# A decoder trunk in fp32 pieces: when the attention stage reads back its softmax weights, its biases and its turned heads

## The chip, the cores and the metric

One core of one Trainium2 chip runs the whole program. The metric is the device time of one launch, in microseconds (us); of several runs the median counts. Beside it stands one profiled execution, from which every busy time and every wait below comes.

## What is computed

The reference is a decoder trunk over 256 tokens of 2048 channels: a gated linear attention layer, a gated feed-forward layer with a short causal convolution, a softmax attention layer that reads shared keys and values, and a second feed-forward layer. The change lies in the third part, which with 256 tokens is plain causal attention over one block (16 heads of 128 channels):

```python
kv = rms_norm(x, norm_w) @ w_kv
k, v = jnp.split(kv, 2, axis=-1)
k = rms_norm(k.reshape(B, S, H, Dh), k_norm_w)
...
q = (rms_norm(x, norm_w) @ w_q).reshape(B, S, H, Dh)
q = (rms_norm(q, q_norm_w) * (Dh ** -0.5)).transpose(0, 2, 1, 3)
...
s_own = jnp.einsum('bhqd,bhkd->bhqk', q_c, k_own).astype(jnp.float32)
s_own = s_own + bias_table[:, rel_bucket(dist_own)][None]
s_own = jnp.where(dist_own >= 0, s_own, -jnp.inf)
p = jax.nn.softmax(scores, axis=-1)
o = einsum(p, v)                  # then  o @ w_out  and the residual
```

## The kernel before

**Weights in two parts, one step at a time.** All products are fp32 and are made from pieces: every weight tile `w` is split into `whi` (ScalarE, L140) and `wlo = w - whi` (VectorE, L141). `WeightStream` holds the list of all weight tiles in the order of use. `step()` hands out the next 128x1024 tile; a counter `cur` counts these steps, and it is the clock of the whole program. In the attention stage a step is 12 matmuls of 512 columns: 8 with `whi` (L290) and 4 with `wlo` (L293). `whi` and `wlo` have three buffers each, so the splits run at most a few steps ahead of TensorE.

**Side work is hung on the step counter.** `after(n, job)` puts a job into a list that `step()` empties when `cur` has come `n` steps further. Jobs that are due at the same step run in the order in which they were entered. `ws.behind()` places what a job issues on ScalarE and VectorE behind the newest weight split in that engine's queue. What the text of the program leaves open is decided when it is compiled: each engine gets one fixed queue of instructions, and an instruction that writes a new tile has its place in the queue only where a buffer for it is there.

**Slots.** One pool, `big`, has 35 buffers ("slots") of 4 KB per partition. Nearly all that lives longer than a moment is in it: the operands `xkv` (8), the four `bias` tiles, the turned heads `q0`, `q1`, `k0`, `k1`, the evacuated products `hsq`, `q`, `k`, `vm0`, `vm1`, the tiles `z` and `turned` of the transposition, the softmax weights `p0`, `p1`, the outputs `ox`.

**The attention stage** has 96 steps of products, counted here from its start:

- steps 0 to 31, query heads, four groups of eight steps (four heads each); steps 32 to 63, key heads, four groups; steps 64 to 95, values, four groups. Each group sums in one of three PSUM tiles `acc`. After it comes the product with the output weights, `mo`.
- A query or key group is evacuated by `head_norm` (L876 to L884: two squares and two scaled copies on ScalarE, a reduction on VectorE, a power on GpSimd, a product), transposed in 32x32 blocks (L384), stored to DRAM (`store`, L387, on GpSimd's DMA queue) and read back turned (`load`, L393, four DMAs). This is `turned(...)`, and `through(g, z, jobs)` times it: the store 1 step after the group, the load 2 steps after, and the reading job 8 steps after. That job is `features` (L892, L896, L303, L304): it makes the operands `q0`, `q1` or `k0`, `k1`.
- `softmax(hd)` for the heads of key group g is due 10 + i steps after the group: scores on TensorE (L908, L910), bias, maximum, exponential, sum, scaling, and block transposition. Two heads make a pair, and a pair goes through DRAM as well: store, load 2 steps after, and `spread_weights` 8 and 9 steps after, which makes `p0` and `p1` (L303, L304, L938).
- `v_out` evacuates a value group (L360, L361, L367), `values(v, p)` (L371 to L374) multiplies the weights of pair p with the values, 3 and 4 steps after the group, and splits the result into `ox` (L303, L304). For pairs 1 and 3, which the output product takes in a form with seven products in place of eight, it also copies the result (`ow`, L956) and makes four sums of its parts (`combine`, L603 to L606, and a split).
- The biases come from a small product (`bias_inputs`, `bias_rows`) that is written to DRAM, and four loads of 512 KB (`bias_load`, L866), at steps 6, 13, and 20, 24, 28, 32. Loads of `hf` (L970) and the operands `xkv` are due at steps 18 to 21 and 26 to 33.

GpSimd's DMA queue carries all of these stores and loads, and GpSimd computes the powers between them; a DMA that has to wait holds up what is behind it. The weights come by SyncE's queue.

Of the kernel before, what the change touches and what calls it, by code (L numbers as in the profile page):

```python
# [8 lines left out]
F32 = mybir.dt.float32  # L9
# [9 lines left out]
S = 256  # L19
# [138 lines left out]
def trunk(ctx: ExitStack, tc: tile.TileContext, xT, x_tok, cst, msk, w1p, w2a, w_k, w_qa, w_v2, w_v, w_g, w_go,  # L158
# [14 lines left out]
    def slot(shape, dt, name):  # L173
        return big.tile(shape, dt, name=name, tag="slot")

    def temp(name, shape=(128, 2, S), dt=F32):
        return tmp.tile(list(shape), dt, name=name, tag="temp")
# [8 lines left out]
    ws = WeightStream(tc, raw, parts)  # L186
# [18 lines left out]
    kqw = keep.tile([128, 1], F32, name="kqw")  # L205
# [60 lines left out]
    cur = [0]  # L266
    later = []

    def after(steps, job):
        later.append((cur[0] + steps, job))  # L270
# [84 lines left out]
    xs = rows(nrm.xs)  # L355
# [7 lines left out]
    def v_out(v, ps, n):  # L363

        r0, r1 = (n.col[:, t:t + 1] for t in range(2))
        split_rows(v[0], ps[:, 0, :], r0)
        A.activation(v[1], ps[:, 1, :], AF.Copy, scale=r1)  # L367
# [8 lines left out]
    def turned(name, groups, a=4, t=2):  # L376

        scratch_ = dram.tile([groups, 4, 32, 4, a * t * 32], F32, name=name)

        def fresh():  # L380
            return slot([128, 4, a, t, 32], F32, "z")

        def square(z, src, t):
            V.transpose(z[:, :, :, t].rearrange("p q a c -> p a q c"), src.rearrange("p (a q c) -> p a q c", q=4, c=32))  # L384

        def store(g, z):
            nc.gpsimd.dma_start(scratch_[g].rearrange("i r q x -> (i r) (q x)"),  # L387
                                z.rearrange("p q a t c -> p (q a t c)"))

        def load(g):  # L390
            f = slot([128, 4, a * t * 32], F32, "turned")
            for q in range(4):
                nc.gpsimd.dma_start(f[32 * q:32 * q + 32], scratch_[g][:, :, q].rearrange("i r x -> r i x"))  # L393
            return f.rearrange("p i (a t c) -> p a t i c", a=a, t=t)

        def through(g, z, jobs):
            got = {}
            after(1, lambda: store(g, z))
            after(2, lambda: got.update(f=load(g)))

            def run(job):
                with ws.behind():
                    job(got["f"])

            for lag, job in jobs:
                after(lag, lambda job=job: run(job))

        return fresh, square, through
# [66 lines left out]
    for hd in (2, 3):  # L475
        ps = gemm_tok(xs)
# [66 lines left out]
    fresh, square, through = turned("keys", 2)  # L543
    for g in range(2):
        z = gemm_tok(xs, 1, lambda ps: evacuated(ps, nrm.col))
# [42 lines left out]
    fresh, square, through = turned("queries", 2)  # L588
    for g in range(2):
        z = gemm_tok(xs, 1, lambda ps: evacuated(ps, col16))  # L590
        jobs = []
# [7 lines left out]
    def combine(k, halves_, into):  # L599

        (a0, a1), (b0, b1) = halves_
        t = temp("comb", (128, 4, 128))
        V.tensor_add(t[:, 0], a1, b1)  # L603
        V.tensor_sub(t[:, 1], t[:, 0], a0)
        V.tensor_sub(t[:, 2], a0, a1)
        V.tensor_sub(t[:, 3], b0, t[:, 1])  # L606
        c = slot([128, 4, 2, 128], F32R, "comb")
        split(c[:, :, 0], c[:, :, 1], t)
        into[k] = c
# [253 lines left out]
    def bias_load(g):  # L863
        t = slot([128, 4, S], F32, "bias")
        s = bscr[:]
        nc.gpsimd.dma_start(t, bass.AP(tensor=s.tensor, offset=s.offset + 4 * g * 384,  # L866
                                       ap=[[1, 128], [384, 4], [1, S]]))
        bias.append(t)
# [21 lines left out]
    def features(x, f, scale, t0):  # L890

        A.activation(f[0].rearrange("p a (i c) -> p a i c", i=4), x[:, :, 0], AF.Copy, scale=scale)  # L892
        for c in range(2):
            w = temp("feat", (128, 2, S - 128 * t0))
            for i in range(2):
                A.activation(w[:, i].rearrange("p (t i c) -> p t i c", i=4, c=32), x[:, 2 * c + i, t0:], AF.Copy,  # L896
                             scale=scale)
            split(f[1][c][:, :, 0, :], f[1][c][:, :, 1, :], w)
# [5 lines left out]
    def softmax(hd):  # L904
        (q0, q1), (k0, k1) = qf[hd // 4], kf[hd // 4]
        q1, k1 = q1[hd // 2 % 2][:, hd % 2], k1[hd // 2 % 2][:, hd % 2]
        sp = bank("s", (128, 384))
        T.matmul(sp[:, 0:128], q0[:, hd % 4, :], k0[:, hd % 4, :], start=True, stop=True)  # L908
        for i, (a, b) in enumerate(((0, 0), (0, 1), (1, 0))):
            T.matmul(sp[:, 128:384], q1[:, a, :], k1[:, b, :], start=i == 0, stop=i == 2)  # L910
        s = temp("s", (128, 384))
        st = small.tile([128, 4], F32, name="st")
        bt = bias[hd // 4][:, hd % 4, :]
        for t, (c0, c1) in enumerate(((0, 128), (128, 384))):
            n = c1 - c0
            rev = bass.AP(tensor=bt.tensor, offset=bt.offset + n - 1, ap=[bt.ap[0], [-1, n]])
            V.tensor_tensor_reduce(s[:, c0:c1], sp[:, c0:c1], rev, -1.0, 3.0e38, OP.add, OP.min,
                                   st[:, t:t + 1])
            A.activation(s[:, c0:c1], s[:, c0:c1], AF.Exp, bias=st[:, t:t + 1], scale=-1.0,
                         accum_out=st[:, 2 + t:3 + t])  # L920
        V.reciprocal(st[:, 2:4], st[:, 2:4])
        for t, (c0, c1) in enumerate(((0, 128), (128, 384))):
            V.tensor_scalar(s[:, c0:c1], s[:, c0:c1], st[:, 2 + t:3 + t], None, op0=OP.mult)
        if hd % 2 == 0:
            pts.append(prob_z())
        prob_square(pts[-1], s, hd % 2)
        if hd % 2:
            prob_through(hd // 2, pts[-1], [(8 + i, lambda f, i=i: spread_weights(hd - 1 + i, f[:, :, i]))
                                            for i in range(2)])

    def spread_weights(hd, f):
        if hd % 8 == 0:
            p1s.append(slot([128, 8, 128], F32, "p1"))
        if hd % 2 == 0:
            p0s.append(slot([128, 2, 2, S], F32R, "p0"))
        hi, lo = (p0s[-1][:, hd % 2, i].rearrange("p (a i c) -> p a i c", a=2, i=4) for i in range(2))
        split(hi, lo, f[:, :2])
        A.copy(p1s[-1][:, hd % 8].rearrange("p (i c) -> p i c", i=4), f[:, 2])  # L938
# [3 lines left out]
    def values(v, p):  # L942
        if p < 6:
            op = bank("o", (128, 2, S))
        else:
            lent[:] = lent or acc_pair()
            op = lent.pop(0)
        for i in range(2):
            hd = 2 * p + i
            p0 = p0s[p][:, i]  # L950
            mix(op[:, i, :], v, (hd % 4) * 128, p0[:, 0], p0[:, 1], p1s[hd // 8][:, hd % 8])
        o = slot([128, 2, 2 * S], F32R, "ox")
        split(o[:, :, :S], o[:, :, S:], op)
        if p in sevens("mo"):
            w = temp("ow")
            A.copy(w, op)  # L956
            combine(p, [(w[:, i, :128], w[:, i, 128:]) for i in range(2)], ox_sums)
        ox.append(o)

    xkv = []  # L960
    after(6, bias_inputs)
    after(13, bias_rows)
    for g in range(4):
        after(20 + 4 * g, lambda g=g: bias_load(g))
    hf = []

    def fetch(m):
# [9 lines left out]
    for g in range(4):  # L977
        z = gemm_tok(xs, 1, lambda ps: head_norm(ps, "q"))
        if g % 2 == 0:
            q8 = slot([128, 8, 128], F32, "q0")  # L980
        q1 = slot([128, 4, 2, 128], F32R, "q1")
        f = (q8[:, g % 2 * 4:g % 2 * 4 + 4], (q1[:, 0:2], q1[:, 2:4]))
        qf.append(f)
        head_through(g, z, [(8, lambda x, f=f: features(x, f, 1.0, 1))])
    xs = rows(xkv)
    for g in range(4):
        z = gemm_tok(xs, 1, lambda ps: head_norm(ps, "k"))
        if g % 2 == 0:
            k8 = slot([128, 8, 128], F32, "k0")
        f = (k8[:, g % 2 * 4:g % 2 * 4 + 4], [slot([128, 2, 2, S], F32R, f"k1{c}") for c in range(2)])  # L990
        kf.append(f)
        head_through(4 + g, z, [(8, lambda x, f=f: features(x, f, kqw, 0))])
        for i in range(4):
            after(10 + i, lambda i=i, g=g: softmax(4 * g + i))
    for g in range(4):
        ps = gemm_tok(xs)
        if g % 2 == 0:
            vm1 = slot([128, 2, 512], F32, "vm1")
        v = (slot([128, 2, 512], F32R, "vm0"), vm1[:, g % 2, :])
        v_out(v, ps, n_q)  # L1000
        for c in range(2):
            after(3 + c, lambda v=v, p=2 * g + c: values(v, p))

# [108 lines left out]
```

## Time and profile before

| | us |
|---|---|
| median of 3 runs | 2206.23 |
| the three runs | 2205.48, 2206.23, 2217.24 |
| the profiled execution, its own time | 2213.89 |
| its span, first to last instruction | 2212.1 |
| TensorE busy in the span | 2180.5 |
| VectorE, ScalarE, GpSimd busy | 1596.1, 1283.9, 300.0 |

The profiled execution has 1.8 us outside its span, and it took 7.66 us more than the median of the three runs. In a timeline, a row gives the start, the length, the engine, the line, the operation with `out<-in`, how many instructions are merged in the row, and in brackets how long the engine had been idle and what ended that. "PE" is TensorE's matmuls, "ACT" ScalarE, "DVE" VectorE, "POOL" GpSimd. The attention stage's first query matmul starts at 1098.34 us, the first key matmul at 1195.36, the first value matmul at 1292.56, and the last one ends at 1388.82.

### The profile page before, as it was taken

The numbers are of one execution on the slowest core, as the hardware profiler recorded it, in microseconds if no ns is written. First come the engines' busy times: TensorE is split into PE (matmuls) and PEld (weight loads), VectorE is DVE, ScalarE is ACT, GpSimd is POOL, SyncE is SP. The second block draws the span as 40 slices with busy tenths as digits, with TensorE's granted clock in tenths as the row PEclk, the third lists the DMA queues.
The fourth block names the chain that finished last, engine by engine and source line by source line (L and its number), as shares of the span: only waits on it lengthen the run. The fifth ranks groups of instructions, "written<-read, shape, count | busy, mean of one in ns | idle before, by whom it ended". The sixth has DMA issues, their size and how long they took to land. (4 is left out here: it accounts for less than half of the span.)

```text
span 2212.1 us, 26963 instructions
## 1 busy us (share of the span) xinstructions
PE 2180.5 (99%) x9693; PEld 1798.9 (81%) x9693; DVE 1596.1 (72%) x2190; ACT 1283.9 (58%) x1856; POOL 300.0 (14%) x448
## 2 busy tenths in 40 slices
PE   9999999999999999999999999899999999999999
PEld 7888887888888888788887788788888888887787
DVE  6655677677777677978767677776777776779886
ACT  6555665555556565555466566555565565655554
POOL 1011111111111111010023231011111111110000
PEclk9999999999999999999999999999999999999999
DMA  8466577677787878576668677486777777775655
GB/s 314 175 228 209 192 243 244 212 233 250 230 254 237 246 238 244 183 245 222 225 229 305 214 253 235 167 259 203 239 244 235 250 242 241 237 246 190 229 209 171
DMA packets 92105, 510.11 MB, mean 231 GB/s; under 512 B 13714, under 2 KB 14754, under 8 KB 41923
## 3 DMA queue, kind: packets, MB, share of 16 engines
q1 hardware_dynamic: 60578, 417.53, 54.8%
q0 software_dynamic: 30816, 90.28, 15.3%
q8 instruction: 76, 1.25, 0.2%
q10 hardware_dynamic: 576, 0.58, 0.1%
q14 instruction: 59, 0.48, 0.1%
HBM read 463.22 MB, written 45.11 MB: 230 GB/s over the span
## 5 line engine op out<-in xcount | busy, mean ns | idle before, releaser
L141 DVE TENSOR_TENSOR wlo<-wraw,whi 128x1024 fp32r<-128x1024 f32 (+1 forms) x786 | 929.6, 1191 | 450.7 <-ACT whi L140 425.2
L140 ACT CAST whi<-wraw 128x1024 fp32r<-128x1024 f32 (+1 forms) x786 | 798.7, 1026 | 668.4 <-PE acc L290 425.0
L290 PE MATMUL acc<-whi,xw 128*128 128x512 f32 x3840 | 954.6, 390 | 3.6 <-ACT whi L140 3.1
L290 PEld LDWEIGHTS acc<-whi,xw 128*128 128x128 f32 x3840 | 721.7, 188 | 155.3 <-ACT whi L140 4.6
L293 PE MATMUL acc<-wlo,xw 128*128 128x512 f32 x1920 | 515.7, 390 | 0.0
L293 PEld LDWEIGHTS acc<-wlo,xw 128*128 128x128 f32 x1920 | 361.1, 188 | 75.1
L728 PE MATMUL acc<-whi,hid 128*128 128x512 f32 x572 | 182.5, 391 | 2.8 <-DVE c L769 2.0
L728 PE MATMUL p<-whi,hid 128*128 128x512 f32 x506 | 166.3, 390 | 0.0
L290 PE MATMUL acc<-whi,xkv 128*128 128x512 f32 x512 | 130.6, 394 | 5.1 <-ACT whi L140 5.1
L667 POOL DMA_DIRECT2D upT<-turned x176 | 114.3, 656 | 145.5 <-DMA turned<-z 56.7
L140 ACT CAST whi<-t 128x1024 fp32r<-128x1024 f32 x82 | 85.6, 1051 | 74.4 <-PE p L728 40.1
L728 PEld LDWEIGHTS acc<-whi,hid 128*128 128x128 f32 x572 | 106.8, 188 | 26.8 <-DVE c L769 2.9
L661 POOL DMA_DIRECT2D turned<-z x44 | 34.2, 776 | 679.4 <-DVE z L657 632.5
L290 PEld LDWEIGHTS acc<-whi,xkv 128*128 128x128 f32 x512 | 96.2, 190 | 25.4 <-ACT whi L140 6.0
L728 PE MATMUL acc<-whi,comb 128*128 128x512 f32 x328 | 108.0, 394 | 5.0 <-ACT whi L140 5.0
L676 ACT ACTIVATE au<-upT,cs 128x256 f32<-128x256 f32 x176 | 96.0, 595 | 27.1 <-DMA upT<-turned 26.9
L728 PEld LDWEIGHTS p<-whi,hid 128*128 128x128 f32 x506 | 94.9, 188 | 19.7
L141 DVE TENSOR_TENSOR wlo<-t,whi 128x1024 fp32r<-128x1024 f32 x82 | 99.0, 1218 | 5.8 <-ACT whi L140 4.4
L728 PE MATMUL acc<-wlo,hid 128*128 128x512 f32 x286 | 94.9, 391 | 2.0 <-DVE wlo L141 2.0
L680 DVE SCALAR_TENSOR_TENSOR au<-upT,cs,au 128x255 f32<-128x255 f32 x176 | 77.2, 472 | 16.3 <-ACT au L676 16.1
L728 PE MATMUL p<-wlo,hid 128*128 128x512 f32 x253 | 83.6, 389 | 0.0
L760 POOL DMA_DIRECT2D c<-rows x24 | 21.2, 1053 | 450.7 <-DVE c L755 438.5
(251 smaller groups left out, 1952.8 us busy)
## 6 DMA issues: line engine op xcount, KB each, us to landing
wraw<-w_up SPq DMA_DIRECT2D x176, 1024.0 KB, 5.3
wraw<-w_dn SPq DMA_DIRECT2D x88, 1024.0 KB, 5.0
turned<-z POOLq DMA_DIRECT2D x44, 512.0 KB, 3.5
upT<-turned POOLq DMA_DIRECT2D x176, 128.0 KB, 5.1
wraw<-w_g SPq DMA_DIRECT2D x16, 1024.0 KB, 5.3
wraw<-w_go SPq DMA_DIRECT2D x16, 1024.0 KB, 6.5
wraw<-w_mq SPq DMA_DIRECT2D x16, 1024.0 KB, 5.8
wraw<-w_kk SPq DMA_DIRECT2D x16, 1024.0 KB, 6.6
```

What stands on the lines that cost most here:

```text
L140: one = nc.scalar.copy(hi[:, a:b], src[:, a:b])
L141: two = nc.vector.tensor_sub(lo[:, a:b], src[:, a:b], hi[:, a:b].bitcast(F32))
L290: T.matmul(ps[:, t, :], xs(kt)[:, x0 + 128 * t:x0 + 128 * t + 128], hi[:, c:c + 512], start=kt == 0 and x0 == 0, stop=False)
L293: T.matmul(ps[:, t, :], xs(kt)[:, 128 * t:128 * t + 128], lo[:, c:c + 512], start=False, stop=kt == KT - 1)
L661: nc.gpsimd.dma_start(turned[J].rearrange("(a i) r q c -> (i r) a (q c)", a=4), z.rearrange("p (a q) t c -> p a (q t c)", a=4))
L667: nc.gpsimd.dma_start(f[32 * q:32 * q + 32].rearrange("p a (i c) -> p (a i) c", i=4), turned[J][:, :, q, :].rearrange("a r c -> r a c"))
L676: A.activation(au[:, i, :], t[:, i, :], AF.Identity, bias=col(cb + n), scale=col(cw + 2 * 2 * FT + n))
L680: V.scalar_tensor_tensor(au[:, i, 1:], t[:, i, :S - 1], col(cw + 2 * FT + n), au[:, i, 1:], op0=OP.mult, op1=OP.add)
L728: T.matmul(p[n], x[xi], w[wi][:, 512 * f:512 * f + 512], start=n not in begun, stop=left[n] == 0)
L760: nc.gpsimd.dma_start(r[n], res(n // 2, 2 * b + n % 2), accum_op=OP.add)
```

## The change

Every operation stays; what changes is when some of them are due, and the pool of one tile.

1. `through` takes the step of the load as an argument. Softmax pairs are now loaded 10 steps before the step at which `values` needs them and spread 4 and 3 steps before it (`use`). With the softmax two steps later (below), pair p of key group g is due to be stored at step 54 + 8g or 56 + 8g, loaded at 65 + 8g or 66 + 8g, spread from 71 + 8g or 72 + 8g, and used at 75 + 8g or 76 + 8g.
2. The biases: inputs at step 18 in place of 6, the product at 25 in place of 13, the four loads at 42, 50, 58, 66 in place of 20, 24, 28, 32.
3. Turned query heads are read 11 steps after their group in place of 8, turned key heads 10 steps after in place of 8, and the softmax starts 12 steps after the key group in place of 10.
4. A value group is evacuated inside `gemm_tok`, ahead of the next weight splits, in place of behind them. The tiles `vm0` and `vm1` are named before the product.
5. The copy `ow` takes a slot in place of one of the six `temp` buffers, and the four sums of pairs 1 and 3 come two steps later, behind the newest weight split.

```diff
-        def through(g, z, jobs):
+        def through(g, z, jobs, fetch=2):
             got = {}
             after(1, lambda: store(g, z))
-            after(2, lambda: got.update(f=load(g)))
+            after(fetch, lambda: got.update(f=load(g)))
...
         if hd % 2:
-            prob_through(hd // 2, pts[-1], [(8 + i, lambda f, i=i: spread_weights(hd - 1 + i, f[:, :, i]))
-                                            for i in range(2)])
+            use = values_at[0] + 8 * (hd // 4) + hd // 2 % 2 - cur[0]
+            prob_through(hd // 2, pts[-1], [(use - 4 + i, lambda f, i=i: spread_weights(hd - 1 + i, f[:, :, i]))
+                                            for i in range(2)], use - 10)
...
         if p in sevens("mo"):
-            w = temp("ow")
+            w = slot([128, 2, S], F32, "ow")
             A.copy(w, op)
-            combine(p, [(w[:, i, :128], w[:, i, 128:]) for i in range(2)], ox_sums)
+
+            def sums():
+                with ws.behind():
+                    combine(p, [(w[:, i, :128], w[:, i, 128:]) for i in range(2)], ox_sums)
+
+            after(2, sums)
         ox.append(o)

     xkv = []
-    after(6, bias_inputs)
-    after(13, bias_rows)
+    values_at = [cur[0] + 64 + 8 + 3]
+    after(18, bias_inputs)
+    after(25, bias_rows)
     for g in range(4):
-        after(20 + 4 * g, lambda g=g: bias_load(g))
+        after(42 + 8 * g, lambda g=g: bias_load(g))
...
-        head_through(g, z, [(8, lambda x, f=f: features(x, f, 1.0, 1))])
+        head_through(g, z, [(11, lambda x, f=f: features(x, f, 1.0, 1))])
...
-        head_through(4 + g, z, [(8, lambda x, f=f: features(x, f, kqw, 0))])
+        head_through(4 + g, z, [(10, lambda x, f=f: features(x, f, kqw, 0))])
         for i in range(4):
-            after(10 + i, lambda i=i, g=g: softmax(4 * g + i))
+            after(12 + i, lambda i=i, g=g: softmax(4 * g + i))
     for g in range(4):
-        ps = gemm_tok(xs)
         if g % 2 == 0:
             vm1 = slot([128, 2, 512], F32, "vm1")
         v = (slot([128, 2, 512], F32R, "vm0"), vm1[:, g % 2, :])
-        v_out(v, ps, n_q)
+        gemm_tok(xs, 1, lambda ps: v_out(v, ps, n_q))
         for c in range(2):
             after(3 + c, lambda v=v, p=2 * g + c: values(v, p))
```

## The prediction

> **What bounds the kernel now.** The page's busy times come first.
>
> ```profile
> span 2212.1 us, 26963 instructions
> PE 2180.5 (99%) x9693; PEld 1798.9 (81%) x9693; DVE 1596.1 (72%) x2190; ACT 1283.9 (58%) x1856; POOL 300.0 (14%) x448
> ```
>
> TensorE is busy for all but 31.6 us of the span, and no matmul is added or taken out. So the change can give back only time in which TensorE stood still or ran slowly, and only in the attention stage, which it touches. The second view is the list of TensorE's waits, cut to the value and output part of that stage (total, number, longest):
>
> ```profile
> PE o L371 <- ACT vm L360: 3.9, 2, 3.5
> PE p L728 <- DVE ox L304: 0.6, 1, 0.6
> PE p L728 <- DVE wlo L141: 0.5, 1, 0.5
> PE o L373 <- DVE vm L361: 0.4, 1, 0.4
> PE acc L374 <- ACT vm L367: 0.3, 1, 0.3
> PE o L374 <- ACT vm L367: 0.2, 1, 0.2
> ```
>
> These are 5.9 us, nearly all of it for values that came late out of PSUM. The third view is TensorE's timeline over the query and key groups, and beside it one key group of eight steps without a stop, as the windows show it:
>
> ```profile
> 1195.36:1217.12 21.76, 21.76 (x98) 18.02 (x96) 18.25 (x27) 16.07 (x29) 5.44 (x6) 1.00 0.78 271
> ```
> ```profile
> 1179.98 2.73 PE L290 MATMUL acc<-whi,xw 128*128 128x512 f32 x8 [2.38 <-ACT whi L140]
> 1184.22 2.22 PE L290 MATMUL acc<-whi,xw 128*128 128x512 f32 x8
> 1187.20 1.98 PE L290 MATMUL acc<-whi,xw 128*128 128x512 f32 x8
> ...
> 1228.60 2.12 PE L290 MATMUL acc<-whi,xkv 128*128 128x512 f32 x8 [0.45 <-ACT whi L140]
> 1231.46 1.98 PE L290 MATMUL acc<-whi,xkv 128*128 128x512 f32 x8
> ...
> 1252.63 3.55 PE L290 MATMUL acc<-whi,xkv 128*128 128x512 f32 x8 [4.69 <-ACT whi L140]
> 1257.08 1.98 PE L290 MATMUL acc<-whi,xkv 128*128 128x512 f32 x8
> ```
>
> A clean step takes 21.76 / 8 = 2.72 us. Three times TensorE waits for a weight split: 2.38, 0.45 and 4.69 us, together 7.52. After a stop it is also slow: the steps from 1179.98, 1184.22, 1228.60 and 1252.63 take 4.24, 2.98, 2.86 and 4.45 us, which is 1.52 + 0.26 + 0.14 + 1.73 = 3.65 us over a clean pace. The two together are 11.2 us. The fourth view, ScalarE's timeline, says why the split was late:
>
> ```profile
> 1177.57 0.63 ACT L892 ACTIVATE q<-turned 128x512 f32<-128x512 f32 x1 [5.62 <-DMA turned<-heads]
> ...
> 1226.19 0.63 ACT L892 ACTIVATE q<-turned 128x512 f32<-128x512 f32 x1 [5.05 <-DMA turned<-heads]
> ...
> 1247.64 1.70 ACT L896 ACTIVATE feat<-turned,kqw 128x256 f32<-128x256 f32 x4 [7.16 <-DMA turned<-heads]
> ```
>
> Each stop of TensorE follows a read of turned heads for which ScalarE stood still, with the next weight splits queued behind it. Three buffers of weights hide the first 3 us or so of such a wait, the rest reaches TensorE.
>
> The last view is when products leave PSUM. TensorE starts the group behind the last key group at 1292.56, and the one behind the first value group at 1316.26:
>
> ```profile
> 1292.56 1.98 PE L290 MATMUL acc<-whi,xkv 128*128 128x512 f32 x8
> ```
> ```profile
> 1316.26 1.98 PE L290 MATMUL acc<-whi,xkv 128*128 128x512 f32 x8
> ```
> ```profile
> 1317.62 0.68 ACT L876 ACTIVATE hsq<-acc,col_n 128x512 f32<-128x512 f32 x1
> ```
> ```profile
> 1351.99 0.68 ACT L360 ACTIVATE vm<-acc,col_n 128x512 fp32r<-128x512 f32 x1
> ```
> ```profile
> 1319.38 2.19 POOL L393 DMA_DIRECT2D turned<-probs  x4 [6.28 <-issue]
> ...
> 1330.59 2.20 POOL L393 DMA_DIRECT2D turned<-heads  x4 [3.33 <-ACT whi L140]
> ...
> 1354.91 2.29 POOL L393 DMA_DIRECT2D turned<-probs  x4 [6.60 <-DMA probs<-z]
> ```
>
> The evacuations begin 25.1 and 35.7 us after their products were complete, 9 and 13 steps late, and not because ScalarE waited in front of them (their rows have no bracket). Each stands within 3 us of the load of a softmax pair, 1319.38 and 1354.91, and that load is the last slot user before it in the program (due at steps 63 and 71, the evacuations at 64 and 72). I read this as follows: slots are given out in program order, so a load that must wait for its store to land also pushes back every later instruction that takes a slot. The lateness grows from group to group until values are multiplied in the middle of the output product.
>
> **The change part by part.** *Turned heads.* The reads of query heads move 3 steps (3 x 2.72 = 8.16 us) later, those of key heads 2 steps (5.44 us). The query waits of 5.62 and 5.05 us are under 8.16 and go. For the key read, 7.16 us is over 5.44, but its chain also starts sooner:
>
> ```profile
> 1228.58 1.23 DVE L141 TENSOR_TENSOR wlo<-wraw,whi 128x1024 fp32r<-128x1024 f32 x1 [3.41 <-ACT whi L140]
> 1229.73 1.30 DVE L384 STREAM_TRANSPOSE z<-k 128x512 f32<-128x512 f32 x2
> ```
>
> The transposition of this group stood behind a VectorE wait of 3.41 us that came from ScalarE's wait of 5.05. With that gone, the margin is 5.44 + 3.41 - 7.16 = 1.7 us. Against it goes the bias: its load is now due at the same step as the load of the key group (42 + 8g) and stands ahead of it in the queue. Its price lies between nothing, when the queue is waiting for the store anyway, and its whole landing time:
>
> ```profile
> bias<-bscr POOLq DMA_DIRECT2D x4, 512.0 KB, 6.5
> ```
>
> Nearest is the first end, since the key load has to wait for its own store several us after that step. I take 2 us; what remains of the wait is then about 0.3 us, and the buffers hide it. At the other end 4.8 us of wait would remain, up to 2 us of it on TensorE. In the query part the bias loads and the bias product leave the crowded stretch, which can only help the loads of `hf` there; I count nothing. Gain: 11.2 us.
>
> *Pairs kept in DRAM, softmax later.* The pair loads are now due 9 to 12 steps after their store is due, so none waits for its store, and the evacuation behind it keeps its place. What stands ahead of an evacuation now is the load of the key group, due 2 steps after that group. In the rows above it is issued 1330.59 - 1317.62 = 13 us, not quite 5 steps, after its group's evacuation, ahead of the next one at 8 steps. The softmax pairs between them are held to that point, one to three steps late, and they have 19 steps to their use. No operation is added, and GpSimd's queue carries the same stores and loads in another order.
>
> *Values, operand sums.* Evacuated in time, the first six pairs are multiplied inside the value groups (steps 75 to 92), and only the last two fall into the output product, as the program has it. This takes away the waits for `vm`, and the work around them at the low clock:
>
> ```profile
> 1366.54 0.28 PE L371 MATMUL o<-p,vm 128*128 128x256 f32 x1
> ...
> 1367.70 0.39 PE L908 MATMUL s<-k,q 128*128 128x128 f32 x2
> ```
> ```profile
> 1397.83 0.58 PE L371 MATMUL o<-p,vm 128*128 128x256 f32 x1 [3.52 <-ACT vm L360]
> ...
> 1402.69 0.92 PE L728 MATMUL p<-whi,ox 128*128 128x512 f32 x2
> ```
>
> One pair takes 1367.70 - 1366.54 = 1.16 us at the full clock; the two pairs from 1397.83 took 4.86, so 2.5 us were lost. Gain: 5.9 + 2.5 = 8.4 us. Evacuating ahead of the splits puts two ScalarE copies of 0.68 us and one VectorE operation in front of the next split; the buffers of weights hide 1.4 us, and without them it would cost four times that, 5.4 us. The sums two steps later go behind the splits and are due well before the steps of those pairs in the output product; `ow` only changes its pool. Nothing for these.
>
> *The sum.* 11.2 + 8.4 = 19.6 us against the profiled 2213.89, which leaves 2194.3. That execution was 7.66 us over the median of 2206.23. If this excess lies in the very stalls that go, the new median is also about 2194; if it lies elsewhere, 2206.2 - 19.6 = 2186.6. Nothing shown decides it; I take the middle, 2190.4, and add 1.6 us for waits that come up in a stage with other orders in all its queues: 2192.
>
> The clock term can be weighed against the Trainium skill, "TensorE: Matmul & The Clock Gate", section "The HAM clock gate", by which the clock halves only after an idle window of about 3.4 us. The trace disagrees at 1179.98, where a stop of 2.38 us was followed by eight matmuls in 2.73 us in place of 1.98. By that rule the first stop would have no clock term and the sum would be 1.8 us smaller.
>
> **The rivals.** *Only one part comes.* If the late evacuations have another cause than the waiting loads, the values stay late, and 11.2 us remain: 2195.0. The landing times of the turned heads are these:
>
> ```profile
> DMA to landing us min/median/max: 3.2/5.6/10.2
> ```
>
> If the reads still meet one of the late ones, 4.6 us over the median, only the value part remains, 8.4 us: 2197.8. For the first case speaks that my reading rests on coincidences in time; against it, that the load and the evacuation go together in both places. Both cases together: chance 0.28.
>
> *It does not do what it says.* The evacuations are late and the reads wait for the same reason, whatever it is, and the new due steps only shift both: 2206. Against it, the waits of 5 to 7 us are named with their DMA. Chance 0.08.
>
> *Slower: the late pair loads turn into ScalarE waits.* A pair is read 6 steps, 16.3 us, after its load is due, where the store's landing was the only limit before. The landing of pair loads takes at most the last figure of this row, and the four DMAs take 2.2 us to issue (the rows of 1319.38 and 1330.59):
>
> ```profile
> DMA to landing us min/median/max: 2.2/4.4/6.9
> ```
>
> That leaves 7.2 us. If GpSimd's queue is held longer than that in front of the load, ScalarE stops at the read with the weight splits behind it, at the price of the row at 1252.63: a wait of 7.16 us cost 4.69 + 1.73 = 6.4 us. With eight pairs it would take five such stops to be slower by 11 us or more: 2206.2 - 19.6 + 5 x 6.4 = 2218.6. The longest wait of a load in the rows above is 6.60 us, and it was for a store, which is gone. Chance 0.07. The Trainium skill, "DMA: Bandwidth & Descriptors", section "Rules for kernel authors", speaks for this rival: it says to issue a DMA early and wait on it late. No row shows the pairs issued this late.
>
> **How the numbers follow.** A measurement of this kernel can tell about 0.5%, 11 us, from no change; the line is at 2195.2. The forecast, both parts, has 0.57, with 2185 to 2198 for itself. Most of it is below the line (0.50 of 0.57), and of the one-part rival about 0.09: faster 0.59. Slower 0.07, and the rest, 0.34, is within 0.5%. The range 2184 to 2206 takes in the one-part rival and the case without effect, and leaves out the slower rival and the tails.
>
> **What would show it.** Right: no stop of TensorE over 1 us between the first query group and the output product; the three waits for `turned<-heads` gone or under 3 us; each key and value group evacuated within 3 us of its last matmul; pair loads with no wait for `probs<-z`; six of the eight pairs multiplied before the output product begins; a granted clock of 1.00 there. Wrong: evacuations still tens of us late would refute the reading of the slots; waits of `p<-turned` on ScalarE would be the slower rival; a clean stage with an unchanged median would mean that the runs around the old median never had these stops.

## The result, and the profile after

The changed kernel takes 2194.64 us (median of 7 runs, 2188.47 to 2201.65), the kernel before beside it 2208.45 us (7 runs, 2204.59 to 2217.24); the ratio is 0.9935, with a 95% interval of 0.9911 to 0.9959. Predicted were 2192.0 us and a range of 2184 to 2206. The profiled execution of the changed kernel took 2194.64 us itself, 19.25 us less than the profiled one of before.

The page of the changed kernel begins so:

```profile
span 2192.9 us, 26952 instructions
...
PE 2171.7 (99%) x9693; PEld 1793.4 (82%) x9693; DVE 1593.7 (73%) x2190; ACT 1283.0 (59%) x1856; POOL 301.1 (14%) x448
```

TensorE's time without work fell from 31.6 to 21.2 us and its busy time by 8.8 us, with the same 9693 matmuls: they ran at a higher clock (mean granted clock 0.998 in place of 0.996). The list of TensorE's waits between the first query group and the end of the output product had seven kinds, 13.4 us; it now has one row (total, number, longest):

```profile
PE p L728 <- DVE wlo L141: 0.5, 1, 0.5
```

Two windows of the stage, around the key groups and the output product, show first the length of the window, then the busy time of TensorE's matmuls, of its weight loads, of VectorE, ScalarE and GpSimd, and behind them the granted clock, which was 0.98 and 0.92 in the same windows of before:

```profile
1195.40:1292.40 97.00, 97.00 (x448) 80.94 (x447) 75.38 (x132) 66.17 (x121) 30.19 (x35) 1.00 0.76 261
...
1388.80:1430.00 41.20, 40.62 (x188) 33.15 (x187) 31.40 (x37) 23.69 (x34) 4.69 (x6) 1.00 0.71 233
```

ScalarE's timeline has the reads of turned heads without a bracket, so without a wait, all but one; that one is the fourth key group's:

```profile
1176.79 0.63 ACT L892 ACTIVATE q<-turned 128x512 f32<-128x512 f32 x1
...
1239.86 1.72 ACT L896 ACTIVATE feat<-turned,kqw 128x256 f32<-128x256 f32 x4
...
1314.34 0.72 ACT L892 ACTIVATE k<-turned,kqw 128x512 f32<-128x512 f32 x1 [1.63 <-DMA turned<-heads]
```

The evacuations of the last key group and the first value group, against the first matmul of the group behind each:

```profile
1284.75 1.98 PE L290 MATMUL acc<-whi,xkv 128*128 128x512 f32 x8
...
1308.90 1.98 PE L290 MATMUL acc<-whi,xkv 128*128 128x512 f32 x8
```
```profile
1285.16 0.68 ACT L876 ACTIVATE hsq<-acc,col_n 128x512 f32<-128x512 f32 x1
...
1310.17 0.68 ACT L360 ACTIVATE vm<-acc,col_n 128x512 fp32r<-128x512 f32 x1
```

They begin 0.4 and 1.3 us late, where it was 25.1 and 35.7. GpSimd's queue shows what the order costs now: the load of those key heads comes 10 us behind its store, and ahead of the store stand two pairs (the rows left out are the second) and a bias.

```profile
1291.26 2.23 POOL L393 DMA_DIRECT2D turned<-probs  x4
1293.48 0.77 POOL L866 DMA_DIRECT2D bias<-bscr  x1
...
1298.52 0.56 POOL L387 DMA_DIRECT2D heads<-z  x1 [0.24 <-DVE wlo L141]
1308.53 1.65 POOL L393 DMA_DIRECT2D turned<-heads  x3 [9.45 <-ACT s L919]
```

### The profile page after: what moved, and what is told of

Read it like the earlier page. It is cut to its first block, busy times and chain, and to the rows that moved or that the text cites. A ratio compares the mean times of both kernels' runs of the same rounds, so it can differ in the third digit from the quotient of the medians.

```text
span 2192.9 us, 26952 instructions
## 1 busy us (share of the span) xinstructions
PE 2171.7 (99%) x9693; PEld 1793.4 (82%) x9693; DVE 1593.7 (73%) x2190; ACT 1283.0 (59%) x1856; POOL 301.1 (14%) x448
## 4 chain that ended last, share of the span: by engine, by line
PE 86%; issue 10%; DMA 3%; DVE 1%; ACT 0%; POOL 0%; SPq 0%; ACTq 0%; POOLq 0%; DVEq 0%
PE acc L290 45%; PE acc L293 22%; PE acc L728 10%; PE p L728 6%; DMA wraw<-w_go 1%; DMA c<-rows 1%; ACT whi L140 0%; PE sT L561 0%; PE o L578 0%; DMA wraw<-w_v 0%; DVE wlo L141 0%; PE acc L793 0%; PE s L910 0%; POOL upT L667 0%; DMA gn<-cst 0%
## 5 line engine op out<-in xcount | busy, mean ns | idle before, releaser
L760 POOL DMA_DIRECT2D c<-rows x24 | 21.2, 1052 | 466.9 <-DVE c L755 454.9
```

The costliest lines, as they stand in the source:

```text
L760: nc.gpsimd.dma_start(r[n], res(n // 2, 2 * b + n % 2), accum_op=OP.add)
```

## The experiments

Ratios are to the kernel before, run beside each on the same chip. "Stops" are TensorE's stops of over 0.15 us in the profiled execution, first in the 96 steps, then in the output product, summed from its timeline. "Stage" is, in the same execution, the time from the first query matmul to the first matmul of the feed-forward layer behind the output product (in the kernel before from 1098.34 to 1493.99 us), so it holds the slow matmuls behind the stops as well. "Late" is how long after the next group's first matmul the first evacuation copy begins, for the last key group (k3) and the first two value groups (v0, v1).

| kernel | ratio, 95% interval | own time, us | stage, us | stops, us | late k3, v0, v1, us |
|---|---|---|---|---|---|
| before | 1 | 2213.89 | 395.7 | 7.5 / 6.0 | 25, 36, 48 |
| the changed kernel | 0.9935 (0.9911 to 0.9959) | 2194.64 | 374.4 | 0 / 0.5 | 0.4, 1.3, 6 |
| heads later, alone | 0.9972 (0.9955 to 0.9989) | 2201.07 | 384.2 | 0 / 6.3 | 24, 36, 48 |
| pair load at 4, alone | 0.9971 (0.9952 to 0.9991) | 2206.89 | 381.3 | 4.9 / 0.5 | 12, 20, 25 |
| these two | 0.9928 (0.9906 to 0.9949) | 2199.75 | 373.8 | 0 / 0.5 | 9, 14, 22 |
| own tiles, alone | 0.9952 (0.9930 to 0.9973) | 2196.40 | 375.3 | 0.9 / 0.5 | 10, 22, 25 |
| softmax at 12, alone | 0.9962 (0.9930 to 0.9995) | 2208.07 | 384.4 | 6.5 / 0.5 | 17, 15, 18 |
| pairs late, alone | 0.9943 (0.9923 to 0.9963) | 2199.63 | 378.6 | 3.5 / 0.8 | 8, 10, 16 |
| changed, load at 2 | 0.9933 (0.9909 to 0.9956) | 2204.80 | 380.8 | 3.5 / 0.5 | 8, 18, 15 |
| the same, biases early | 0.9920 (0.9896 to 0.9944) | 2195.84 | 374.5 | 0 / 0.7 | 7, 12, 13 |
| changed, load at use - 6 | 0.9921 (0.9900 to 0.9942) | 2194.13 | 374.1 | 0 / 0.3 | 0.4, 3, 6 |
| changed, load at use - 5 | 0.9958 (0.9940 to 0.9976) | 2204.58 | 378.9 | 0 / 3.2 | 0.4, 3, 6 |

My theory: two separate causes. ScalarE waits for turned heads, with weight splits queued behind; and a pair's load, which takes a slot and has to wait for its store, holds back every later writer of a slot, so that values come late. The main rivals: one cause for both; a shortage of slots or some other cause of the late evacuations.

### One part, the other, and both

```diff
-        head_through(g, z, [(8, lambda x, f=f: features(x, f, 1.0, 1))])
+        head_through(g, z, [(11, lambda x, f=f: features(x, f, 1.0, 1))])
...
-        head_through(4 + g, z, [(8, lambda x, f=f: features(x, f, kqw, 0))])
+        head_through(4 + g, z, [(10, lambda x, f=f: features(x, f, kqw, 0))])
```

> The kernel before with one part alone: turned query heads are read 11 steps after their group and key heads 10 steps after, in place of 8 and 8; nothing else changes. Theory (two separate causes): the three stops of TensorE for weight splits in the query and key groups (7.5 us of waits, 11.2 us with the slow steps behind them) go, and the late evacuations stay, so value waits of 4 to 6 us with some 2 us of slow clock stay in the output product: ratio to before about 0.995 (11.2 of 2208). Rival (one cause: the late evacuations come from ScalarE's stops at the turned heads): both go, ratio 0.991 to 0.9935, and the key and value groups leave PSUM within 3 us of their last matmul.

```diff
-            after(2, lambda: got.update(f=load(g)))
+            after(4 if name == "probs" else 2, lambda: got.update(f=load(g)))
```

> The kernel before with one number changed: softmax pairs are loaded 4 steps after they are due to be turned, in place of 2; reads of heads, softmax and spreading stay as they are. The load of a group's second pair then stands in the program behind the evacuation of the next group, not ahead of it. Theory (a load that waits for its store holds back the next writer of a slot): the key and value groups leave PSUM in time or one to two steps late, not 9 and 13 steps, value waits and slow clock in the output product go (8.4 us), the stops at the turned heads stay (7.5 us of waits, 11.2 us in all): ratio about 0.996. Rival (slots are short, or another cause than the load's place): evacuations stay 25 and 36 us late, ratio 1.000.

> The two changes above together in the kernel before: heads read at 11 and 10, pairs loaded 4 steps after. Everything else of the change is missing: biases early, softmax at 10, values evacuated behind the splits, operand sums at once, pairs spread early. Theory: these other parts are worth nothing, so the stage is as clean as in the changed kernel, ratio 0.991 to 0.996 like its 0.9935, with under 2 us of TensorE stops between the first query group and the end of the output product. Rival (late loads or the earlier evacuation of values carry a part of it): 3 us or more of stops stay in the output product.

The list of TensorE's waits in the stage, of the first of them, its two largest rows:

```profile
PE o L371 <- ACT vm L360: 4.3, 2, 3.5
PE p L728 <- DVE ox L304: 0.9, 2, 0.8
```

of the second, whole:

```profile
PE acc L290 <- ACT whi L140: 4.9, 3, 4.1
PE p L728 <- DVE wlo L141: 0.5, 1, 0.5
```

and of both together, whole:

```profile
PE p L728 <- DVE wlo L141: 0.5, 1, 0.5
```

Each edit takes away one kind of wait and leaves the other: the first list has no weight splits left, and its evacuations are as late as before; the second has no values left. The causes are separate, and the rival with one cause is out. The first ratio, 0.9972, is nearer to 1 than the 0.995 I had expected; its stage is 11.5 us shorter, near the 11.2 expected. The two numbers give the stage that the whole change gives, 373.8 us against 374.4, at a ratio of 0.9928 against 0.9935. The other parts (biases late, pairs spread late, values evacuated ahead of the splits, `ow` and the sums) move no time that these intervals can tell. My size for the evacuations with the load at 4 was too good: k3 is 12 us late, four steps, not one or two.

### What makes the evacuations late

The load at 4 moved the load in the program. The next kernel leaves it there, and takes from it only the slot:

```diff
+        for _ in range(3):
+            f = slot([128, 4, 192], F32, "turned")
+            nc.gpsimd.memset(f[:, 0, 0:1], 0.0)
+            held.append(f)
...
-            f = slot([128, 4, a * t * 32], F32, "turned")
+            if held:
+                f = held[g % len(held)]
+            else:
+                f = slot([128, 4, a * t * 32], F32, "turned")
```

> The kernel before, where the turned pairs go in turn into three tiles that are taken once, early in the stage, so that a pair's load takes no slot; it stays due 2 steps after the turning, ahead of the next group's evacuation, and head reads stay at 8. One memset of a column for each of the three tiles is added. Theory (taking a slot while waiting for the store is what holds the evacuations back): they are in time or up to three steps late, the value waits of the output product go, the waits for turned heads (7.5 us of TensorE stops) stay, ratio about 0.997 as with the load at 4. Rival (the load's place in GpSimd's queue or its due step itself, not the slot): evacuations stay 25 and 36 us late, ratio 1.000.

GpSimd's timeline and ScalarE's, around the last key group, whose successor starts at 1285.95 us:

```profile
1300.36 2.20 POOL L396 DMA_DIRECT2D turned<-probs  x4 [8.41 <-DMA probs<-z]
...
1306.93 2.23 POOL L396 DMA_DIRECT2D turned<-probs  x4 [1.89 <-ACT whi L140]
```
```profile
1296.18 0.68 ACT L879 ACTIVATE hsq<-acc,col_n 128x512 f32<-128x512 f32 x1
```

The first load stands for 8.41 us waiting for its store, longer than any load of a pair in before, and the evacuation begins in the middle of that wait: ahead of both loads, though both stand ahead of it in the program. In before it came behind the first (1310.36) and beside the second (1319.38). It is 10 us late in place of 25, the first value group 22 in place of 36, and no value wait is left. It is the slot, then, and not the place of the load in GpSimd's queue. Nor do slots run short: compiled with 33 of them in place of 35, and not run, the kernel has every evacuation at the same place of ScalarE's queue as before. The remainder here (I had said three steps at most; the first value group is eight clean steps late) has other causes, which were not sought; no stop of TensorE follows from it.

With the load at 4, a part of what remains can be read from the program and the trace. That edit moves the load of a group's second pair behind the next evacuation, but it also moves the load of the first pair to the step right ahead of it, where the second stood. The evacuation of the last key group begins beside that load:

```profile
1308.23 2.19 POOL L393 DMA_DIRECT2D turned<-probs  x4 [6.11 <-PE acc L290]
```
```profile
1308.21 0.67 ACT L876 ACTIVATE hsq<-acc,col_n 128x512 f32<-128x512 f32 x1
```

Two other parts of the change, each by itself:

```diff
-            after(10 + i, lambda i=i, g=g: softmax(4 * g + i))
+            after(12 + i, lambda i=i, g=g: softmax(4 * g + i))
```

> The kernel before with one part alone: the softmax starts 12 steps after its key group in place of 10; reads of heads at 8, pair loads 2 steps after the turning, biases early. The load of a group's second pair moves from one step ahead of the next group's evacuation to one step behind it. Theory (a load that waits for its store, ahead of an evacuation and taking a slot, delays it): evacuations in time or up to four steps late, no value waits in the output product, the same 5.9 us of waits and 8.4 us in all as with the load at 4: ratio 0.9955 to 0.998; stops at turned heads stay. Rival (it needs the load to be late by itself): evacuations 25 and 36 us late.

The other has the first item of the change alone, `use` and all, with the softmax at 10.

> The kernel before with the first part of the change alone: pairs loaded 10 steps before use and spread 4 and 3 steps before it; softmax at 10, reads of heads at 8, biases early. This is the edit to which the prediction gave the 8.4 us of the value part. Theory: the same 8.4 us as with the load at 4, evacuations in time or up to two steps late, no value waits; the stops at turned heads stay: ratio 0.9955 to 0.998.

The waits of TensorE with the softmax at 12, whole, and then with the pairs late:

```profile
PE acc L290 <- ACT whi L140: 6.5, 3, 5.0
PE p L728 <- DVE wlo L141: 0.5, 1, 0.5
```
```profile
PE acc L290 <- ACT whi L140: 3.5, 2, 2.3
PE p L728 <- DVE wlo L141: 0.5, 1, 0.5
PE acc L373 <- DVE vm L361: 0.3, 1, 0.3
```

Either cures the values by itself. The later softmax puts the load of a group's second pair behind the next evacuation (the first pair's load then stands right ahead of it, as with the load at 4: the last key group's evacuation begins at 1303.97, that load at 1302.78); the late loads put both behind. The ratio of the late loads, 0.9943, is better than the 0.9955 to 0.998 expected; this execution also had smaller stops at the heads than the one of before. So the cures overlap: the load at 4, the later softmax and the late loads each give the value part, and the change, which has the last two, needs one.

### What the late loads are worth beside the later softmax

```diff
-                                            for i in range(2)], use - 10)
+                                            for i in range(2)])
```

> The changed kernel with one part taken back: pairs are loaded 2 steps after they are turned, not 10 steps before their use; they are still spread late. My prediction's working gave the whole cure of the late evacuations to the late loads: by it the waits of the output product return, 8.4 us, ratio 0.9935 + 0.0038 = 0.997. Theory now: with the softmax 2 steps later the load of the second pair stands behind the next evacuation anyway, so nothing returns and the ratio is that of the changed kernel, 0.991 to 0.996, with under 2 us of stops in the stage.

The ratio says nothing returns, but this execution has a new stop, 3.5 us where I had expected under 2 in all. ScalarE and TensorE:

```profile
1324.49 0.72 ACT L892 ACTIVATE k<-turned,kqw 128x512 f32<-128x512 f32 x1 [5.65 <-DMA turned<-heads]
```
```profile
1329.21 3.78 PE L290 MATMUL acc<-whi,xkv 128*128 128x512 f32 x8 [3.46 <-ACT whi L140]
```

and GpSimd's queue ahead of that read:

```profile
1301.75 2.22 POOL L393 DMA_DIRECT2D turned<-probs  x4 [1.19 <-PE acc L293]
1304.62 0.77 POOL L866 DMA_DIRECT2D bias<-bscr  x1 [0.65 <-issue]
1305.38 0.56 POOL L387 DMA_DIRECT2D heads<-z  x1
1315.37 2.20 POOL L393 DMA_DIRECT2D turned<-heads  x4 [9.43 <-DMA heads<-z]
```

The store of the key heads, issued right behind a pair and a 512 KB bias, took over 9 us to land. With the biases early as well:

```diff
-    after(18, bias_inputs)
-    after(25, bias_rows)
+    after(6, bias_inputs)
+    after(13, bias_rows)
     for g in range(4):
-        after(42 + 8 * g, lambda g=g: bias_load(g))
+        after(20 + 4 * g, lambda g=g: bias_load(g))
```

> The changed kernel with the pair loads 2 steps after the turning (as in the run before this one) and with the biases early again (steps 6, 13, 20 to 32). In the run before, the read of the fourth key group's turned heads cost ScalarE 5.65 us and TensorE 3.46 us; ahead of that group's store and load stood a pair load and a bias load of 512 KB. Theory (the late bias load in the queue ahead of the key heads' store makes it late): without it that wait falls by the bias load's landing time, about 6 us, to under 1 us, and TensorE has under 1 us of stops in the stage; ratio 0.990 to 0.995. Rival (the pair loads alone make it late): a wait of 4 us or more for turned heads stays, with 2 us or more of a stop.

```profile
1291.84 1.71 ACT L896 ACTIVATE feat<-turned,kqw 128x256 f32<-128x256 f32 x4 [2.15 <-DMA turned<-heads]
```

TensorE has no stop in the groups, but waits for turned heads stay, this one of 2.15 us and another of 1.6 on ScalarE, not under 1 us as I had said. The load of the last key group's heads waited 3.35 us for its store here and 9.43 us there. That the bias carries a part of the delay is suggested by this pair of executions, not shown: the stops of three executions of one kernel differ as much (below). The interval of either kernel holds the other's ratio, so that the late bias costs time in the median is not shown either.

### How late a pair may come

```diff
-                                            for i in range(2)], use - 10)
+                                            for i in range(2)], use - 6)
```

> The changed kernel with the pair loads 6 steps before use in place of 10, 2 steps (5.4 us) ahead of their reads. This presses on the slower rival of the prediction: four issues of 2.2 us and a landing of 2.2 to 6.9 us, less 5.4, leave waits of ScalarE of minus 1 to 3.7 us at each of 8 pairs. Theory (the weight buffers hide the first 3 us of a wait): TensorE stops under 2 us in all, ratio to before 0.991 to 0.996. Rival (every wait reaches TensorE): up to 8 x 3.7 = 30 us, ratio up to 1.007.

The other has `use - 5` there.

> The changed kernel with the pair loads 5 steps before use, 1 step (2.7 us) ahead of their reads. Four issues of 2.2 us and a landing of 2.2 to 6.9 us, less 2.7, leave waits of 1.7 to 6.4 us of ScalarE at each of 8 pairs, 3.9 us at the median landing. Theory (buffers hide 3 us): 1 us of TensorE stop for each pair at the median and up to 3.4, 8 to 20 us with the slow steps behind them, ratio to before 0.996 to 1.003. Rival (the compiled queue sets the reads later by itself and takes the wait out): no stop, ratio as the changed kernel, 0.991 to 0.996.

With the loads 5.4 us ahead of their reads nothing is lost: TensorE has stops of 0.3 us, and ScalarE waits for a pair once, 1.6 us. With 2.7 us ahead the kernel is slower (the intervals just meet, and its five times, 2202.07 us and more, all lie above the other's four, 2197.71 and less), but not as I had priced it: ScalarE waits for a pair once again, 1.64 us. Instead the compiled queue has the reads of the last two heads later. They now stand between two weight splits of the output product, at 1403.28, which is 114.1 us after the first value matmul; in the changed kernel they begin 108.6 us after it:

```profile
1403.28 0.40 ACT L303 CAST p<-turned 128x256 fp32r<-128x256 f32 x1
...
1404.29 1.04 ACT L140 CAST whi<-t 128x1024 fp32r<-128x1024 f32 x1
```
```profile
1405.38 0.50 PE L728 MATMUL acc<-whi,comb 128*128 128x512 f32 x1 [2.00 <-ACT whi L140]
```

Both sides missed the mechanism: hardly a wait, but no free time either. The medians are 7.9 us apart (2204.58 and 2196.68). The stages of the two profiled executions are 4.8 us apart, 2.9 of it stops and the rest mostly slow matmuls behind them (granted clock 0.69 from 1405.38 to 1409.00); another 4.1 us of this execution were lost ahead of the stage, where the edit changes nothing. So some 3 us of the difference in the medians are not explained.

### The kernel before, twice more

> The kernel before, unchanged, in another profiled execution. Question: how much of the 11.2 us of the feature part belongs to every execution. The part alone was worth 0.28%, 6.2 us, in medians, and other kernels with head reads at 8 had 4.9 and 0.9 us of stops there in place of 7.5. Theory (the landing times differ between executions): 1 to 5 us of stops for weight splits in the query and key groups in this one; the value part is set by the compiled queue and comes again: 5 to 7 us of stops. Rival (the part is the same in each execution): 7 to 8 us of stops for weight splits again.

> The kernel before once more, a third profiled execution, with the same question: theory, 1 to 5 us of stops for weight splits in the query and key groups, and not the same as in the other two; value waits 5 to 7 us again. Rival: 7 to 8 us of stops for weight splits again.

They took 2214.84 and 2216.04 us. The value part is there each time (stops of 5.4 and 6.7 us, evacuations 48 us late at v1). The stops for weight splits are 7.3 us in the first, as the rival had it, and 1.6 us in the second, as the theory had it. The second has another stop, of 4.35 us, in their place. ScalarE, then TensorE:

```profile
1327.10 0.50 ACT L938 COPY p<-turned 128x128 f32<-128x128 f32 x2 [6.94 <-DMA turned<-probs]
```
```profile
1329.22 1.23 PE L908 MATMUL s<-k,q 128*128 128x128 f32 x4 [4.35 <-ACT k L892]
```

Here ScalarE waited for a pair, not for heads. Which read meets a late DMA differs between executions; that some read does was so in all three. The whole stage took nearly the same each time: 395.7, 395.0 and 394.4 us.

## Why the prediction was right, and where it was not

**Right.** The forecast case, both parts, is what came. The three waits for turned heads are gone, the values leave PSUM in time, six pairs are multiplied before the output product, the clock is 1.00. Two details were too sharp: two pair loads still wait for their store, 3.0 us together, and v1 and the last value group leave 6 and 8 us late, not within 3. The sum by the profiled execution, 2213.89 - 19.6 = 2194.3, is the profiled time after within 0.4 us, and that is in part luck: the stage became 395.7 - 374.4 = 21.3 us shorter, and the execution after spent 2 us more outside it, where nothing was changed. The slots given out in program order were a reading of coincidences; the load at 4 and the own tiles show that this is the mechanism.

**The median.** 2192 was 2.6 us too low, and most of that comes from the step behind the sum, in which I held the profiled execution to lie 7.66 us above its median. The three runs shown were low: over 61 runs of the kernel before in four sets the median is 2213.03 (2204.15 to 2229.69), and the profiled time is in their middle. There was no excess to place. That the forecast lies so near is luck as well: beside the changed kernel the one of before took 2208.45 us, so the gain in medians is 13.8 us, not 19.6, which the interval of the ratio (9 to 20 us) just holds.

**The turned heads, a term too large in the median.** 11.2 us were in the profile of before; alone this part measured 0.28%, between 2.4 and 10.0 us of 2212. In single executions it was not too large: the stage with the heads read later took 384.2 us, which is 10.2 to 11.5 us less than the three executions of before. Their stops for weight splits were 7.5, 7.3 and 1.6 us, but in the third the stop at the pair made up for it. So which read stops TensorE is one draw, and the loss was nearly the same three times. But four kernels that read the heads as early and have the values in time have stages of 375.3 to 384.4 us, 1.4 to 10.6 over the 373.8 of the two numbers. Whether the execution or the order of the queues makes that difference, no run here separates. The profiled run with the heads later, 2201.07 us, is the fastest of that kernel's twelve. What else their median of 2204.95 holds, 3.9 us more, no trace shows.

**The values.** 8.4 us predicted; 6.4 us alone with the load at 4 (0.29%, 2 to 11 us), 10.6 with own tiles (0.48%) and 12.6 with the late loads (0.57%, 8 to 17 us), whose profiled runs also had smaller stops at the heads. By the stage, from the heads read later to the two numbers together, it is 384.2 - 373.8 = 10.4 us: the term was some 2 us too small, though 0.5 of its 5.9 us of waits, the one for `wlo`, has nothing to do with values and is there after as before. The price held within these intervals, but I tied it to the late loads. With the softmax at 12, which I had not costed at all, the load of a group's second pair stands behind the evacuation anyway, and the late loads add only punctuality that TensorE doesn't need: v1 may be 25 us late without a stop, and 48 is too late.

**The rivals.** One part alone, and no effect, did not come: each part exists by itself. The slower rival had its price from waits of ScalarE at the reads (the landing times it went by are those of stores and loads together); with the loads 5 steps, 13.6 us, later than in the change, there was one such wait, of 1.64 us. It was the kernel before, with its early loads, that waited 6.94 us for a pair. The Trainium skill, "DMA: Bandwidth & Descriptors", section "Rules for kernel authors", with its rule to issue early and wait late, spoke for that rival. No run here shows its harm down to 5.4 us ahead; what harmed here was an issue so early that it had to wait for its store.

**Nothing for the rest.** Biases, evacuation ahead of the splits, `ow` and sums: confirmed within the interval by the two numbers alone. The bias I had weighed against the read of its own key group; where it could be seen, it was the store of the next heads behind it that was late.

## What to carry to other kernels

When an evacuation is late and its engine did not wait in front of it, look in the program for the last instruction ahead of it that takes a buffer of the same pool and itself waits for something: moving that one behind the evacuation, or giving it a tile of its own, is enough. Look for the smallest edit that gives the same trace: two numbers did here what the whole change did. And cost stops at DMA reads from several executions, and by the length of the whole stage: in the kernel before the stops moved from one read to another, while the stage stayed within 1.3 us.

## What the runs showed of the hardware

The slow matmuls behind a stop don't follow from its length alone. Of two runs of eight matmuls behind stops of nearly the same length, in the kernel with the pairs late and, ahead of the attention stage, in the changed one with the load at 2, the first went at almost the full pace and the second did not (a clean run of eight takes 1.98 us). The granted clock was 1.00 over the first and 0.63 over the second:

```profile
1227.90 2.14 PE L290 MATMUL acc<-whi,xkv 128*128 128x512 f32 x8 [2.26 <-ACT whi L140]
```
```profile
675.52 3.13 PE L290 MATMUL acc<-whi,xw 128*128 128x512 f32 x8 [2.34 <-ACT whi L140]
```

The Trainium skill, "TensorE: Matmul & The Clock Gate", section "The HAM clock gate", has the clock halve after at least one idle window of about 3.4 us, and the window runs freely. That nearly the same stop is priced differently agrees with a window that runs freely; that a stop of 2.34 us is enough does not agree with a whole idle window.
